# HGRN2 recurrence of a streaming encoder step: one chain over all chunks of a half in place of three chains of three chunks

## The chip, the cores and the metric

The kernel runs on one core of one Trainium2 chip. The metric is device time in microseconds (us) of one execution; the time before is the median of three runs. A profiled execution of the same program gives the trace.

## The reference, cut to what matters

One encoder layer works on a prompt of 2048 tokens and on 8 running streams of 16 tokens (128 tokens together). A projection of 1024 to 4096 columns feeds two groups: stick-breaking attention (8 heads of 64) and HGRN2, a gated linear recurrence (4 heads, key and value dimension 128). The change concerns HGRN2 alone:

```python
# per head: f = lb + (1-lb)*sigmoid(fh), k = 1 - f, q = silu(qh)
# S_t = diag(f_t) S_{t-1} + k_t outer i_t,   o_t = S_t^T q_t
def step(S, xs):                       # one chunk
    qc, kc, gc, ic = xs
    b = jnp.cumsum(gc, axis=2)         # gc = log f
    decay = jnp.where(causal, jnp.exp(b[:, :, :, None, :] - b[:, :, None, :, :]), 0.0)
    scores = jnp.einsum('bhtd,bhsd,bhtsd->bhts', qc, kc, decay)
    o = einsum('bhts,bhsv->bhtv', scores, ic) + einsum('bhtd,bhdv->bhtv', qc * exp(b), S)
    S_new = exp(b_last)[..., None] * S + einsum('bhsd,bhsv->bhdv', kc * exp(b_last - b), ic)
    return S_new, o
# then per head RMSNorm of o, times a gain and silu(gh); then the output projection and LayerNorm
```

## The kernel before, in words

The program has two stages. In the first, TensorE computes the whole input projection in two halves of the tokens: half 0 has 1024 prompt tokens and the 128 sample tokens (nine chunks of 128), half 1 the other 1024 prompt tokens (eight chunks). In the second come attention, the running streams and the output projection.

The first stage goes over `order`, a list of sections of the projection: for each head FH, QH, GH (forget gate, query, output gate of HGRN2), a few sections of the attention (KA, QA, VA, GA), and IH (HGRN2's values) for two heads at a time. A section is computed in three tiles of up to 384 tokens, each by 24 matmuls into a PSUM tile `pj` (`pe_T`, lines 311 to 318; `pe_N`, lines 320 to 328, has tokens on the output's partitions). The next section's weights are split into a high and a low part (`split_w`, line 262, called at line 681 when the first tile of a section is done): ScalarE copies, GpSimd subtracts (line 118).

When GH of a head is done (line 688), three chains are queued for it, one for each tile of three chunks (`hgrn`, lines 406 to 553). A chain is a Python generator whose `yield`s cut it into 13 steps (15 with the sample chunk). `weave` (line 608) is called between groups of 6 to 12 projection matmuls, three times a tile in `pe_T`. Each call adds `HRATE` = 1.0 to a credit (kept at 2.0 at most), and each whole credit issues one step of a chain at that place of every engine's program:

```python
credit[0] = min(credit[0] + rate, 2.0)
while credit[0] >= 1.0 and step_chain():
    credit[0] -= 1.0
```

`step_chain` (line 588) takes the first chain, issues one step and puts it back at place 1, so that the two oldest chains alternate. `drain` (line 615) finishes chains whose tiles are about to be used again. Engines run what is issued to them in order, so the places fixed by `weave` set the order of all work.

The steps of a chain: the first computes kS = 1 - f and q times f into a tile `qf` (VectorE) and clears `sc` and `sd` (GpSimd). Then come seven levels, m = 1, 2, 4, ..., 64. At a level TensorE forms products of kS and q in small blocks, 32 columns wide up to m = 16 (`near`, lines 427 to 431; the first level also forms a product `p0` with the q not yet multiplied), pairs of 32 at m = 32 and of 64 at m = 64 (line 451), into a PSUM tile `ps`. VectorE multiplies half of q and half of kS by running products of f (`tot`, lines 467 and 468), takes the scores out of `ps` (`keep`, line 434; line 461) and forms the next `tot` (line 471). The next level's products read the multiplied q and kS. A float32 matmul of the program stands as two records in the trace.

The last part: transposes of kS into `pk`, copied to `kN` (line 482); products of kN with the values into `pu` and the state's update `st`, `stt` (lines 495 to 505); the output `po` from `sc` and from `qf` with the old states (lines 510 to 518); squares on ScalarE (line 522); the root on GpSimd (`rsqrt`, line 131); the scaling on VectorE (line 528); transposes into `pq` and the gate (lines 532 and 533); the store. For the sample chunk, states of eight streams are loaded, read and updated (lines 414, 486, 518, 541 to 553).

Of the kernel before, what the change touches and what calls it, by code (L numbers as in the profile page):

```python
# [41 lines left out]
HRATE = 1.0  # L42
# [24 lines left out]
def stream_step_kernel(ctx: ExitStack, tc: tile.TileContext, x_prompt, x_sample, cache_k, cache_v, state_s,  # L67
# [131 lines left out]
    with ExitStack() as ph:  # L199
# [3 lines left out]
        hw = R("hw", 2)  # L203
# [202 lines left out]
        def hgrn(half, h, hg, t0, nch):  # L406
            n = nch * P
            smp = half == 0 and t0 + n > 1024
            npr = nch - 1 if smp else nch
            c0 = t0 // P  # L410
            q, f, g = (hg[a][:, t0:t0 + n] for a in "qfg")
            iv = lambda c: hg["i"][:, c0 + c]
# [4 lines left out]
            kS = hw.tile([P, TW], F32, name="kS", tag="kS")[:, :n]  # L417
            dve.tensor_scalar(kS, f, -1.0, 1.0, ALU.mult, ALU.add)
            sc = hw.tile([P, 3, P], F32, name="sc", tag="sc")
            sd = hw.tile([P, 3, BLK], F32, name="sd", tag="sd")  # L420
            q0, q = q, hw.tile([P, TW], F32, name="qf", tag="qf")[:, :n]
            pool.memset(sc[:, :nch], 0.0)
            pool.memset(sd[:, :nch], 0.0)
            dve.tensor_tensor(q, q0, f, ALU.mult)
            yield

            def near(ps, q, k):
                for c in range(k):
                    for s0_ in range(0, P, BLK):
                        r = slice(c * P + s0_, c * P + s0_ + BLK)  # L430
                        mm(ps[s0_:s0_ + BLK, c], kS[:, r], q[:, r], start=True, stop=True)  # L431
# [3 lines left out]

            tot = f
            tot16 = None
            for li, m in enumerate(LEVELS):
                k = nch if m < TS else npr
                bank = psc.tile([P, 4, P], F32, name="ps", tag="ps")  # L440
                ps = bank[:, :, :BLK]
                if m < BLK:
                    if li == 0:
                        p0 = bank[:, :, BLK:2 * BLK]
                        near(p0, q0, nch)
                    near(ps, q, k)
                else:
                    ps = bank
                    for c in range(k):
                        for s0_ in range(0, P, 2 * m):  # L450
                            mm(ps[s0_:s0_ + m, c, :m], kS[:, c * P + s0_:c * P + s0_ + m],
                               q[:, c * P + s0_ + m:c * P + s0_ + 2 * m], start=True, stop=True)

                def keep_scores():
                    if m < BLK:
                        if li == 0:
                            keep(p0, NL, nch)
                        keep(ps, li, k)
                        return
                    for s0_ in range(0, P, 2 * m):  # L460
                        dve.tensor_copy(sc[s0_:s0_ + m, :k, s0_ + m:s0_ + 2 * m], ps[s0_:s0_ + m, :k, :m])

                nn = k * P
                q4 = q[:, :nn].rearrange("p (b two m) -> p b two m", two=2, m=m)
                k4 = kS[:, :nn].rearrange("p (b two m) -> p b two m", two=2, m=m)
                t3 = tot[:, :nn // m].rearrange("p (b two) -> p b two", two=2)
                dve.tensor_tensor(q4[:, :, 1], q4[:, :, 1], bc(t3[:, :, 0], m), ALU.mult)
                dve.tensor_tensor(k4[:, :, 0], k4[:, :, 0], bc(t3[:, :, 1], m), ALU.mult)
                keep_scores()
                nt = hw.tile([P, TW // 2 // m], F32, name=f"tot{m}", tag=f"tot{m}")[:, :nn // (2 * m)]  # L470
                dve.tensor_tensor(nt, t3[:, :, 0], t3[:, :, 1], ALU.mult)
                tot = nt
                if m == 8:
                    tot16 = nt
                if m == BLK:
                    for s0_ in range(0, P, BLK):
                        r = slice(s0_, s0_ + BLK)
                        pool.tensor_copy(sc[r, :nch, r], sd[r, :nch])
                yield
            pk = pt.tile([P, 4, P], F32, name="pk", tag="pt")  # L480
            for c in range(nch):
                nc.tensor.transpose(pk[:, c], ch(kS, c), ident)
            kN = hw.tile([P, 3, P], F32, name="kN", tag="kN")
            act.copy(kN[:, :nch], pk[:, :nch])
            if smp:
                qz = xr.tile([P, NB, P], F32, name="qz", tag="x")
                pool.memset(qz[:, :, :2 * TS], 0.0)
                for a in range(2):
                    pool.tensor_copy(qz[:, a::2, a * TS:(a + 1) * TS],
                                     ch(q, npr).rearrange("p (b a t) -> p b a t", a=2, t=TS)[:, :, a])  # L490
            yield
            po = pho.tile([P, 4, P], F32, name="po", tag="po")
            pu = pt.tile([P, 4, P], F32, name="pu", tag="pt")
            for c in range(npr):
                mm(pu[:, c], kN[:, c], iv(c), start=True, stop=True)
            olds = []
            tmp = hw.tile([P, 2, P], F32, name="stt", tag="stt")
            cur = st[h][(c0 // 3 + 3 * half) % 3]
            for c in range(npr):
                olds.append(cur)  # L500
                new = tmp[:, c] if c < npr - 1 else st[h][(c0 // 3 + 3 * half + 1) % 3]
                if half == 0 and c0 + c == 0:
                    dve.tensor_copy(new, pu[:, c])
                else:
                    dve.scalar_tensor_tensor(new, cur, tot[:, c:c + 1], pu[:, c], ALU.mult, ALU.add)
                cur = new
            yield
            for c in range(npr):
                only = half == 0 and c0 + c == 0
                mm(po[:, c], sc[:, c], iv(c), start=True, stop=only)  # L510
                if not only:
                    mm(po[:, c], ch(q, c), olds[c], start=False, stop=True)
            if smp:
                c = npr
                mm(po[:, c], sc[:, c], iv(c), start=True, stop=True)
                for b in [*range(0, NB, 2), *range(1, NB, 2)]:
                    r = slice(b // 2 * 2 * TS, (b // 2 + 1) * 2 * TS)
                    mm(po[r, c], qz[:, b, :2 * TS], s0[:, b], start=False, stop=True, skip_group_check=True)
            ms = hw.tile([P, 4], F32, name="ms", tag="ms")
            mo = hw.tile([P, 3, P], F32, name="mo", tag="mo")  # L520
            for c in range(nch):
                act.activation(mo[:, c], po[:, c], AF.Square, accum_out=ms[:, c:c + 1])
            yield
            rs = hw.tile([P, 4], F32, name="rs", tag="rs")
            rsqrt(rs[:, :nch], ms[:, :nch], 1.0 / DG, RMS_EPS)
            yield
            on = hw.tile([P, 3, P], F32, name="on", tag="on", bufs=1)
            dve.tensor_tensor(on[:, :nch], po[:, :nch], bc(rs[:, :nch], P), ALU.mult)
            yield
            pq = pt.tile([P, 4, P], F32, name="pq", tag="pt")  # L530
            for c in range(nch):
                nc.tensor.transpose(pq[:, c], on[:, c], ident)
            dve.tensor_tensor(mo[:, :nch], pq[:, :nch], g.rearrange("p (c t) -> p c t", t=P), ALU.mult)
            mf = mo.rearrange("p c t -> p (c t)")
            for a, c, m in spans(half, t0, n):
                defer(lambda a=a, c=c, m=m: dma.dma_start(mx_d[4 + h][:, c:c + m], mf[:, a:a + m]), 2)
            if half == 1 and t0 + n == 1024:
                dma.dma_start(s_prompt[0, 0, h], st[h][(c0 // 3 + 3 * half + 1) % 3])
            if smp:
                yield  # L540
                iz = qz[:, :4]
                pool.tensor_tensor(iz, iv(npr).unsqueeze(1).to_broadcast([P, 4, P]), bc(hmask, P), ALU.mult)
                yield
                pbs = []
                for b in range(2):
                    pbs.append(psc.tile([P, 4, P], F32, name="pb", tag="ps"))
                    r = slice(b * DH, (b + 1) * DH)
                    mm(pbs[b], kN[r, npr], iz[r], start=True, stop=True)
                for b in range(NB):
                    pb = pbs[b // 4]  # L550
                    o = npr * P // TS + b
                    dve.scalar_tensor_tensor(s0[:, b], s0[:, b], tot16[:, o:o + 1], pb[:, b % 4], ALU.mult, ALU.add)
# [35 lines left out]
        def step_chain():  # L588
# [4 lines left out]
            if not done:  # L593
                chains.insert(min(1, len(chains)), g)
# [40 lines left out]
        for i, (half, sec, j) in enumerate(order):  # L635
# [52 lines left out]
            if sec == GH:  # L688
                for t0, n in TILES[half]:
                    chains.append((4 * half + j, gen1(hgrn(half, j, hg, t0, n // P))))  # L690
# [624 lines left out]
```

## Time and profile before

| | us |
|---|---|
| median of three runs | 1715.24 |
| lowest and highest run | 1713.12, 1717.34 |
| the profiled execution, its own time | 1714.12 |
| its span on the core | 1712.3 |
| TensorE matmul busy | 1646.8 |
| VectorE busy | 895.5 |
| GpSimd busy | 771.3 |
| ScalarE busy | 700.5 |

The span is the stretch from the first to the last instruction of the trace, and all windows count from its start. Busy time is the union of an engine's instructions; idle time stands with the instruction that ended it and with what that instruction waited for. The first stage reaches to about 980 us.

### The profile page before, as it was taken

The numbers are of one execution on the slowest core, as the hardware profiler recorded it, in microseconds if no ns is written. First come the engines' busy times: TensorE is split into PE (matmuls) and PEld (weight loads), VectorE is DVE, ScalarE is ACT, GpSimd is POOL, SyncE is SP. The second block draws the span as 40 slices with busy tenths as digits, with TensorE's granted clock in tenths as the row PEclk, the third lists the DMA queues.
The fourth block names the chain that finished last, engine by engine and source line by source line (L and its number), as shares of the span: only waits on it lengthen the run. The fifth ranks groups of instructions, "written<-read, shape, count | busy, mean of one in ns | idle before, by whom it ended". The sixth has DMA issues, their size and how long they took to land.

```text
span 1712.3 us, 38577 instructions
## 1 busy us (share of the span) xinstructions
PE 1646.8 (96%) x15413; PEld 1468.1 (86%) x15413; DVE 895.5 (52%) x1738; ACT 700.5 (41%) x1617; POOL 771.3 (45%) x942
## 2 busy tenths in 40 slices
PE   8999999999999999999999879999999999999998
PEld 8999999998989999999989858777787777778886
DVE  4253442245423342531554257788887777765555
ACT  3231221221223221221222257787878888874110
POOL 1242221223331332232333356776776776665664
PEclk9999999999999999999999989999999999999999
DMA  4233232122344242231123596999885854422443
GB/s 157 59 117 104 64 102 75 52 81 63 111 139 138 64 127 59 84 102 41 64 64 108 141 219 133 241 193 223 174 199 148 223 153 124 93 70 68 140 143 112
DMA packets 298811, 204.16 MB, mean 119 GB/s; under 512 B 113532, under 2 KB 275976, under 8 KB 298632
## 3 DMA queue, kind: packets, MB, share of 16 engines
q1 hardware_dynamic: 298632, 201.69, 44.4%
q8 instruction: 123, 2.02, 0.5%
q14 instruction: 56, 0.46, 0.1%
HBM read 146.06 MB, written 56.10 MB: 118 GB/s over the span
## 4 chain that ended last, share of the span: by engine, by line
PE 85%; ACT 5%; DMA 3%; DVE 3%; POOL 1%; issue 1%; SPq 0%; POOLq 0%; DVEq 0%; ACTq 0%
PE pj L314 12%; PE pj L316 10%; PE pj L315 10%; PE po L808 7%; PE z L755 6%; PE wt L790 6%; PE pj L324 4%; PE py L1145 4%; PE pj L326 4%; PE pj L325 4%; PE py L1147 4%; PE py L1146 4%; PE ps L431 2%; PE pk L890 2%; ACT keep L763 1%
## 5 line engine op out<-in xcount | busy, mean ns | idle before, releaser
L314 PE MATMUL pj<-xh,wh 128*128 128x384 f32 (+1 forms) x1152 | 399.3, 347 | 0.0
L316 PE MATMUL pj<-xh,wl 128*128 128x384 f32 (+1 forms) x1152 | 377.8, 328 | 0.0
L315 PE MATMUL pj<-xl,wh 128*128 128x384 f32 (+1 forms) x1152 | 377.3, 328 | 0.0
L777 POOL TENSOR_TENSOR s<-s,pr 128x512 f32<-128x512 f32 (+3 forms) x320 | 322.8, 1014 | 119.9 <-DVE pr L724 101.5
L118 POOL TENSOR_TENSOR wl<-wr,wh 128x512 fp32r<-128x512 f32 x126 | 164.3, 1327 | 345.6 <-ACT wh L110 320.7
L724 DVE TENSOR_TENSOR_SCAN pr<-keep,pr,one 128x513 f32<-128x513 f32 x192 | 238.4, 1269 | 49.5 <-ACT keep L763 35.9
L314 PEld LDWEIGHTS pj<-xh,wh 128*128 128x128 f32 x1152 | 217.9, 189 | 9.1 <-issue 2.9
L315 PEld LDWEIGHTS pj<-xl,wh 128*128 128x128 f32 x1152 | 218.6, 190 | 0.0
L316 PEld LDWEIGHTS pj<-xh,wl 128*128 128x128 f32 x1152 | 217.8, 189 | 0.0
L755 PE MATMUL z<-kst,qr 128*128 128x512 f32 (+3 forms) x640 | 186.5, 402 | 16.5 <-ACT keep L763 6.5
L110 ACT COPY wh<-wt 128x512 f32<-128x512 f32 (+3 forms) x320 | 166.1, 551 | 79.2 <-PE wt L790 77.9
L760 ACT ACTIVATE s<-z 128x512 f32<-128x512 f32 (+3 forms) x320 | 185.6, 580 | 12.6 <-PE z L757 9.2
L790 PE MATMUL wt<-ident,s 128*128 128x128 f32 x1088 | 166.0, 280 | 4.3 <-POOL s L777 3.9
L324 PE MATMUL pj<-wh,xh 128*128 128x256 f32 x544 | 162.1, 298 | 0.0
L790 PEld LDWEIGHTS wt<-ident,s 128*128 128x128 f32 x1088 | 124.0, 143 | 36.8 <-issue 15.5
L325 PE MATMUL pj<-wl,xh 128*128 128x256 f32 x544 | 153.7, 283 | 0.0
L326 PE MATMUL pj<-wh,xl 128*128 128x256 f32 x544 | 153.7, 283 | 0.0
L808 PEld LDWEIGHTS po<-wh,vst 128*64 128x64 f32 x2176 | 118.4, 138 | 26.1 <-issue 16.5
L118 POOL TENSOR_TENSOR e<-ev,e 128x384 fp32r<-128x384 f32 (+1 forms) x48 | 44.4, 926 | 210.7 <-ACT e L110 156.8
L755 PEld LDWEIGHTS z<-kst,qr 128*128 128x128 f32 x640 | 105.1, 196 | 38.0 <-ACT keep L763 18.6
L808 PE MATMUL po<-wh,vst 128*64 128x128 f32 x2176 | 137.7, 278 | 0.0
L763 ACT ACTIVATE keep<-z 128x512 f32<-128x512 f32 (+2 forms) x230 | 135.4, 589 | 0.0
(160 smaller groups left out, 2683.6 us busy)
## 6 DMA issues: line engine op xcount, KB each, us to landing
wr<-in_w_in SPq DMA_DIRECT2D x64, 512.0 KB
qr<-qT_d SPq DMA_DIRECT2D x64, 256.0 KB
kr<-in_cache_k SPq DMA_DIRECT2D x16, 1024.0 KB
vr<-in_cache_v SPq DMA_DIRECT2D x32, 512.0 KB
kst<-kT_d SPq DMA_DIRECT2D x24, 512.0 KB
mt<-mx_d SPq DMA_DIRECT2D x136, 64.0 KB
x<-in_x_prompt SPq DMA_DIRECT2D x16, 512.0 KB
out<-xr SPq DMA_DIRECT2D x16, 512.0 KB
```

The costliest lines, as they stand in the source:

```text
L118: eng_lo.tensor_tensor(lo, src, f32(hi), ALU.subtract)
L314: mm(o, wh[:, k], xh[:, k, :n], start=k == 0, stop=False)
L315: mm(o, wh[:, k], xl[:, k, :n], start=False, stop=False)
L316: mm(o, wl[:, k], xh[:, k, :n], start=False, stop=k == KT - 1)
L324: mm(o, xh[:, k, ts], wh[:, k], start=k == 0, stop=False)
L325: mm(o, xh[:, k, ts], wl[:, k], start=False, stop=False)
L326: mm(o, xl[:, k, ts], wh[:, k], start=False, stop=k == KT - 1)
L724: dve.tensor_tensor_scan(pr[:, CW - wd:CW + 1][:, ::-1], kr, by, carry, ALU.mult, ALU.bypass)
L755: mm(z[:, :wd], q[:, a, r, q0:q0 + P], k[:, a, k0:k0 + wd], start=r == 0, stop=r == 1 and not top)
L777: pool.tensor_tensor(s[:, :wd], s[:, :wd], pr[:, CW - wd + 1:CW + 1], ALU.mult)
L790: nc.tensor.transpose(pt_[:, x:x + P], U[(u, a)][0][:, x:x + P], ident)
L808: mm(o[r], v[:, lo // P % 8 + x, r], th[a][:, x * P:(x + 1) * P], start=top and x == 0, stop=bot and x == n - 1, skip_group_check=True)
```

## The change

Each head of each half gets one chain over all its chunks (nine in half 0, eight in half 1), where it had three chains of three chunks (the last of two in half 1). Each level is then one run of products over all chunks, and each VectorE and GpSimd instruction of a level covers all chunks. The product with the unmultiplied q gets a step of its own ahead of the levels. The last part goes in groups of three chunks in five stages (`back`, `state`, `read`, `scale`, `gate`), each group one step behind the one before it. Tiles are overwritten: q takes the place of `qf`, kS of `kN`, `sc` of `mo` and `on`, the gate tile `g` takes the output; the pool `hw` has one buffer of a tile where it had two. `step_chain` puts the chain back at the front, so that one chain is worked on until it is done. A chain has 17 steps, and `HRATE` goes from 1.0 to 0.45. The core of the diff:

```diff
-HRATE = 1.0
+HRATE = 0.45
...
-        hw = R("hw", 2)
+        hw = R("hw")
...
-        def hgrn(half, h, hg, t0, nch):
+        def hgrn(half, h, hg, nch):
             n = nch * P
...
-            kS = hw.tile([P, TW], F32, name="kS", tag="kS")[:, :n]
+            kS = hw.tile([P, 9 * P], F32, name="kS", tag="kS")[:, :n]
             dve.tensor_scalar(kS, f, -1.0, 1.0, ALU.mult, ALU.add)
...
-            dve.tensor_tensor(q, q0, f, ALU.mult)
-            yield
...
+            ps = bank(BLK)
+            near(ps, nch)
+            dve.tensor_tensor(q, q, f, ALU.mult)
+            keep(ps, NL, nch)
+            yield
             tot = f
             tot16 = None
             for li, m in enumerate(LEVELS):
                 k = nch if m < TS else npr
-                bank = psc.tile([P, 4, P], F32, name="ps", tag="ps")
-                ps = bank[:, :, :BLK]
+                ps = bank(max(m, BLK))
                 if m < BLK:
-                    if li == 0:
-                        p0 = bank[:, :, BLK:2 * BLK]
-                        near(p0, q0, nch)
-                    near(ps, q, k)
+                    near(ps, k)
...
+            groups = [(c, min(c + 3, nch)) for c in range(0, nch, 3)]
...
+            stages = (back, state, read, scale, gate)
+            for j in range(len(groups) + len(stages) - 1):
...
+                for i, (c0, c1) in enumerate(groups):
+                    if 0 <= j - i < len(stages):
+                        stages[j - i](i, c0, c1)
+                yield
...
-                chains.insert(min(1, len(chains)), g)
+                chains.insert(0, g)
...
-                for t0, n in TILES[half]:
-                    chains.append((4 * half + j, gen1(hgrn(half, j, hg, t0, n // P))))
+                chains.append((4 * half + j, gen1(hgrn(half, j, hg, 9 - half))))
```

`bank(m)` is a PSUM tile of 512 columns seen as chunks of m columns. `back` transposes three chunks of kS and copies them over kS (ScalarE); `state` has the products into `pu` and the update; `read` the output, its squares and the root (`rsqrt`) in one step; `scale` the multiplication on VectorE; `gate` the transposes, the gate and the store.

## Rows read from the trace of the kernel before

**Rows 1.** The page: busy time of all engines, and the granted TensorE clock in 40 equal slices of the span (tenths of full speed).
```profile
PE 1646.8 (96%) x15413; PEld 1468.1 (86%) x15413; DVE 895.5 (52%) x1738; ACT 700.5 (41%) x1617; POOL 771.3 (45%) x942
...
PEclk9999999999999999999999989999999999999999
```
**Rows 2.** Busy time by stretch of the span: length, then busy us and instructions of each engine, granted clock, DMA share, GB/s.
```profile
0.00:100.00 100.00, 94.09 (x829) 90.50 (x830) 37.99 (x93) 28.61 (x52) 20.42 (x27) 1.00 0.35 108
100.00:980.00 880.00, 862.92 (x8685) 812.22 (x8683) 347.02 (x1026) 202.90 (x526) 258.20 (x368) 1.00 0.30 90
980.00:1150.00 170.00, 153.02 (x1495) 125.77 (x1496) 122.61 (x148) 121.72 (x281) 114.71 (x153) 0.93 0.91 196
1150.00:1712.00 562.00, 536.79 (x4408) 439.63 (x4406) 387.88 (x472) 347.27 (x760) 377.95 (x394) 0.99 0.55 144
```
**Rows 3.** What TensorE waited for from 0 to 980 us: who for whom, us in total, times, longest.
```profile
PE ps L431 <- DVE kS L468: 7.2, 8, 1.0
PE xT L305 <- DMA x<-in_x_prompt: 5.7, 2, 5.2
PE pq L532 <- DVE on L528: 2.6, 3, 1.3
PE ps L431 <- DVE sd L434: 2.3, 2, 1.1
PE pb L548 <- POOL qz L542: 1.7, 1, 1.7
```
**Rows 4.** Timeline of TensorE around one run of small products (level m = 2, three chunks, 12 matmuls, 24 records): start us, us, instruction, count.
```profile
200.80 0.33 PE L315 MATMUL pj<-xl,wh 128*128 128x384 f32 x1
200.97 0.34 PE L316 MATMUL pj<-xh,wl 128*128 128x384 f32 x1
201.24 0.40 PE L431 MATMUL ps<-qf,kS 128*32 128x32 f32 x24
201.56 0.45 PE L314 MATMUL pj<-xh,wh 128*128 128x384 f32 x1
201.85 0.34 PE L315 MATMUL pj<-xl,wh 128*128 128x384 f32 x1
```
**Rows 5.** The same around a run of a first level, 48 records in one run.
```profile
84.11 0.34 PE L316 MATMUL pj<-xh,wl 128*128 128x384 f32 x1
84.38 0.39 PE L431 MATMUL ps<-hq,kS 128*32 128x32 f32 x24
84.59 0.42 PE L431 MATMUL ps<-qf,kS 128*32 128x32 f32 x24
84.94 0.44 PE L314 MATMUL pj<-xh,wh 128*128 128x384 f32 x1
85.22 0.34 PE L315 MATMUL pj<-xl,wh 128*128 128x384 f32 x1
```
**Rows 6.** Groups of TensorE instructions from 0 to 980 us, shapes apart: the small products of all levels up to m = 16 with qf (count, busy us, mean ns, idle before).
```profile
L431 PE MATMUL ps<-qf,kS 128*32 128x32 f32 x2688 | 46.5, 200 | 9.5 <-DVE kS L468 7.2 <-DVE sd L434 2.3
```
**Rows 7.** Timeline of TensorE around a run of level m = 64 (three chunks, 64 columns wide).
```profile
108.60 0.34 PE L316 MATMUL pj<-xh,wl 128*128 128x384 f32 x1
108.87 0.56 PE L451 MATMUL ps<-qf,kS 128*64 128x64 f32 x6
109.36 0.45 PE L314 MATMUL pj<-xh,wh 128*128 128x384 f32 x1
```
**Rows 8.** Timeline of TensorE around the transposes of kS (three chunks, all 128 columns).
```profile
112.60 0.34 PE L316 MATMUL pj<-xh,wl 128*128 128x384 f32 x1
112.79 0.49 PE L482 MATMUL pk<-ident,kS 128*128 128x128 f32 x3
113.03 0.42 PE L314 MATMUL pj<-xh,wh 128*128 128x384 f32 x1
113.29 0.33 PE L315 MATMUL pj<-xl,wh 128*128 128x384 f32 x1
```
**Rows 9.** Groups of VectorE instructions from 0 to 985 us, shapes apart: q times f, and kS = 1 - f (count, busy us, mean ns).
```profile
L424 DVE TENSOR_TENSOR qf<-hq,hf 128x384 f32<-128x384 f32 x20 | 11.0, 552 | 0.0
...
L418 DVE TENSOR_SCALAR kS<-hf 128x384 f32<-128x384 f32 x20 | 7.0, 351 | 0.0
...
L424 DVE TENSOR_TENSOR qf<-hq,hf 128x256 f32<-128x256 f32 x4 | 1.7, 419 | 0.0
```
**Rows 10.** Timeline of VectorE: one multiplication of q at a level, three chunks.
```profile
203.95 0.34 DVE L467 TENSOR_TENSOR qf<-qf,tot 128x192 f32<-128x192 f32 x1
```
**Rows 11.** Timelines from 252 to 259 us, of GpSimd (four subtractions of a weight split), VectorE (the two multiplications of a level) and TensorE (the next run, with its idle time).
```profile
251.70 5.24 POOL L118 TENSOR_TENSOR wl<-wr,wh 128x512 fp32r<-128x512 f32 x4
...
252.01 1.20 DVE L467 TENSOR_TENSOR qf<-qf,tot 128x192 f32<-128x192 f32 x1 [1.14 <-PE ps L431]
253.14 1.42 DVE L468 TENSOR_TENSOR kS<-kS,tot 128x192 f32<-128x192 f32 x1
...
254.71 0.40 PE L431 MATMUL ps<-qf,kS 128*32 128x32 f32 x24 [1.01 <-DVE kS L468]
```
**Rows 12.** Timeline of VectorE and TensorE where the first chain of a head begins: kS, and the ninth projection matmul of the section behind GH.
```profile
82.42 0.35 DVE L418 TENSOR_SCALAR kS<-hf 128x384 f32<-128x384 f32 x1
82.55 0.33 PE L316 MATMUL pj<-xh,wl 128*128 128x384 f32 x1
```

More of the change, by code (lines that the diff above doesn't have):

```diff
@@ L403, in v_store @@
             dma.dma_start(v_prompt[0, 0, 2 * j:2 * j + 4, r0:r0 + P].rearrange("h t d -> t h d"), v3)
-        def hgrn(half, h, hg, t0, nch):
+        def hgrn(half, h, hg, nch):
             n = nch * P
[L408 to L412, printed above, removed]
+            npr = 8
+            smp = nch > npr
+            q, f, g = (hg[a][:, :n] for a in "qfg")
+            iv = lambda c: hg["i"][:, c]
             ch = lambda a, c: a[:, c * P:(c + 1) * P]
@@ L416, in hgrn, with bank, near @@
                 dma.dma_start(s0, state_s[0, :, h].rearrange("b d e -> d b e"))
-            kS = hw.tile([P, TW], F32, name="kS", tag="kS")[:, :n]
+            kS = hw.tile([P, 9 * P], F32, name="kS", tag="kS")[:, :n]
             dve.tensor_scalar(kS, f, -1.0, 1.0, ALU.mult, ALU.add)
-            sc = hw.tile([P, 3, P], F32, name="sc", tag="sc")
-            sd = hw.tile([P, 3, BLK], F32, name="sd", tag="sd")
-            q0, q = q, hw.tile([P, TW], F32, name="qf", tag="qf")[:, :n]
+            sc = hw.tile([P, 9, P], F32, name="sc", tag="sc")
+            sd = hw.tile([P, 9, BLK], F32, name="sd", tag="sd")
+            pool.memset(sd[:, :nch], 0.0)
             pool.memset(sc[:, :nch], 0.0)
-            pool.memset(sd[:, :nch], 0.0)
-            dve.tensor_tensor(q, q0, f, ALU.mult)
             yield
-            def near(ps, q, k):
+            def bank(m):
+                return psc.tile([P, 512], F32, name="ps", tag="ps").rearrange("p (c j) -> p c j", j=m)
+            def near(ps, k):
                 for c in range(k):
@@ L439, in hgrn @@
                 k = nch if m < TS else npr
-                bank = psc.tile([P, 4, P], F32, name="ps", tag="ps")
-                ps = bank[:, :, :BLK]
+                ps = bank(max(m, BLK))
                 if m < BLK:
-                    if li == 0:
-                        p0 = bank[:, :, BLK:2 * BLK]
-                        near(p0, q0, nch)
-                    near(ps, q, k)
+                    near(ps, k)
                 else:
-                    ps = bank
                     for c in range(k):
                         for s0_ in range(0, P, 2 * m):
-                            mm(ps[s0_:s0_ + m, c, :m], kS[:, c * P + s0_:c * P + s0_ + m],
+                            mm(ps[s0_:s0_ + m, c], kS[:, c * P + s0_:c * P + s0_ + m],
                                q[:, c * P + s0_ + m:c * P + s0_ + 2 * m], start=True, stop=True)
[L454 to L461, printed above, removed]
                 nn = k * P
@@ L468, in hgrn @@
                 dve.tensor_tensor(k4[:, :, 0], k4[:, :, 0], bc(t3[:, :, 1], m), ALU.mult)
-                keep_scores()
-                nt = hw.tile([P, TW // 2 // m], F32, name=f"tot{m}", tag=f"tot{m}")[:, :nn // (2 * m)]
+                if m < BLK:
+                    keep(ps, li, k)
+                else:
+                    for s0_ in range(0, P, 2 * m):
+                        dve.tensor_copy(sc[s0_:s0_ + m, :k, s0_ + m:s0_ + 2 * m], ps[s0_:s0_ + m, :k])
+                nt = hw.tile([P, 9 * P // 2 // m], F32, name=f"tot{m}", tag=f"tot{m}")[:, :nn // (2 * m)]
                 dve.tensor_tensor(nt, t3[:, :, 0], t3[:, :, 1], ALU.mult)
@@ L479, in hgrn @@
                 yield
[L480 to L484, printed above, removed]
-            if smp:
[L486 to L490, printed above, removed]
@@ L491, in hgrn @@
-            yield
[L492 to L543, printed above, removed]
+            groups = [(c, min(c + 3, nch)) for c in range(0, nch, 3)]
+            cur = [st[h][half * len(groups) % 3]]
+            olds, pos, rss = {}, {}, {}
+            def back(i, c0, c1):
+                pk = pt.tile([P, 4, P], F32, name="pk", tag="pt")
+                for c in range(c0, c1):
+                    nc.tensor.transpose(pk[:, c - c0], ch(kS, c), ident)
+                act.copy(kS[:, c0 * P:c1 * P].rearrange("p (c d) -> p c d", d=P), pk[:, :c1 - c0])
@@ new lines, in state @@
+            def state(i, c0, c1):
+                pu = pt.tile([P, 4, P], F32, name="pu", tag="pt")
+                c1 = min(c1, npr)
+                for c in range(c0, c1):
+                    mm(pu[:, c - c0], ch(kS, c), iv(c), start=True, stop=True)
+                tmp = hw.tile([P, 2, P], F32, name="stt", tag="stt", bufs=2)
+                for c in range(c0, c1):
+                    olds[c] = cur[0]
+                    new = tmp[:, c - c0] if c < c1 - 1 else st[h][(half * len(groups) + i + 1) % 3]
+                    if half == 0 and c == 0:
+                        dve.tensor_copy(new, pu[:, 0])
+                    else:
+                        dve.scalar_tensor_tensor(new, cur[0], tot[:, c:c + 1], pu[:, c - c0], ALU.mult, ALU.add)
+                    cur[0] = new
@@ new lines, in read @@
+            def read(i, c0, c1):
+                po = pos[i] = pho.tile([P, 4, P], F32, name="po", tag="po")
+                for c in range(c0, c1):
+                    o = po[:, c - c0]
+                    only = half == 0 and c == 0
+                    mm(o, sc[:, c], iv(c), start=True, stop=only or c == npr)
+                    if c == npr:
+                        for b in [*range(0, NB, 2), *range(1, NB, 2)]:
+                            r = slice(b // 2 * 2 * TS, (b // 2 + 1) * 2 * TS)
+                            mm(o[r], qz[:, b, :2 * TS], s0[:, b], start=False, stop=True, skip_group_check=True)
+                    elif not only:
+                        mm(o, ch(q, c), olds[c], start=False, stop=True)
+                ms = hw.tile([P, 4], F32, name="ms", tag="ms", bufs=2)
+                for c in range(c0, c1):
+                    act.activation(sc[:, c], po[:, c - c0], AF.Square, accum_out=ms[:, c - c0:c - c0 + 1])
+                rs = rss[i] = hw.tile([P, 4], F32, name="rs", tag="rs", bufs=2)
+                rsqrt(rs[:, :c1 - c0], ms[:, :c1 - c0], 1.0 / DG, RMS_EPS)
@@ new lines, in scale, with gate @@
+            def scale(i, c0, c1):
+                dve.tensor_tensor(sc[:, c0:c1], pos[i][:, :c1 - c0], bc(rss[i][:, :c1 - c0], P), ALU.mult)
+            def gate(i, c0, c1):
+                pq = pt.tile([P, 4, P], F32, name="pq", tag="pt")
+                for c in range(c0, c1):
+                    nc.tensor.transpose(pq[:, c - c0], sc[:, c], ident)
+                mo = g[:, c0 * P:c1 * P]
+                m3 = mo.rearrange("p (c t) -> p c t", t=P)
+                dve.tensor_tensor(m3, pq[:, :c1 - c0], m3, ALU.mult)
+                for a, c, m in spans(half, c0 * P, (c1 - c0) * P):
+                    defer(lambda a=a, c=c, m=m: dma.dma_start(mx_d[4 + h][:, c:c + m], mo[:, a:a + m]), 2)
+                if half == 1 and c1 == npr:
+                    dma.dma_start(s_prompt[0, 0, h], cur[0])
@@ new lines, in hgrn @@
+            stages = (back, state, read, scale, gate)
+            for j in range(len(groups) + len(stages) - 1):
+                if j == 0 and smp:
+                    qz = xr.tile([P, NB, P], F32, name="qz", tag="x")
+                    pool.memset(qz[:, :, :2 * TS], 0.0)
+                    for a in range(2):
+                        pool.tensor_copy(qz[:, a::2, a * TS:(a + 1) * TS],
+                                         ch(q, npr).rearrange("p (b a t) -> p b a t", a=2, t=TS)[:, :, a])
+                if j == 5 and smp:
+                    iz = qz[:, :4]
+                    pool.tensor_tensor(iz, iv(npr).unsqueeze(1).to_broadcast([P, 4, P]), bc(hmask, P), ALU.mult)
+                for i, (c0, c1) in enumerate(groups):
+                    if 0 <= j - i < len(stages):
+                        stages[j - i](i, c0, c1)
+                yield
@@ L547, in hgrn @@
                     r = slice(b * DH, (b + 1) * DH)
-                    mm(pbs[b], kN[r, npr], iz[r], start=True, stop=True)
+                    mm(pbs[b], ch(kS, npr)[r], iz[r], start=True, stop=True)
                 for b in range(NB):
-                    pb = pbs[b // 4]
                     o = npr * P // TS + b
-                    dve.scalar_tensor_tensor(s0[:, b], s0[:, b], tot16[:, o:o + 1], pb[:, b % 4], ALU.mult, ALU.add)
+                    dve.scalar_tensor_tensor(s0[:, b], s0[:, b], tot16[:, o:o + 1], pbs[b // 4][:, b % 4],
+                                             ALU.mult, ALU.add)
                 defer(lambda: dma.dma_start(s_sample[0, :, h].rearrange("b d e -> d b e"), s0), 2)
```

## The prediction

> **What bounds the kernel now.** I read the page first: TensorE is busy for 96% of the span, VectorE for 52%, at the full granted clock nearly throughout [rows 1]. Then the busy time by stretch, since an average hides stages [rows 2]. From 100 to 980 us, where the chains of HGRN2 run beside the projection, TensorE is busy 862.9 of 880 us at clock 1.00; VectorE stands at 347, GpSimd at 258, ScalarE at 203, DMA at a share of 0.30. This stage is TensorE's alone: what shortens its in-order program by a microsecond shortens the stage by about one, and work taken from the others gives nothing by itself. The change touches only this stage. From 980 to 1150 us DMA is at 0.91, but these loads are issued behind the first stage, so that they move with its end. Third, who TensorE waits for up to 980 us [rows 3]: the chains make it wait 7.2 + 2.3 + 2.6 + 1.7 = 13.8 us; 5.7 us are for x at the two starts and stay.
>
> "Busy" says nothing of what a run of small products costs, so I read the timeline around single runs. Projection matmuls start 0.17 us apart (200.80, 200.97). A run of 24 records sits between the matmul at 200.97 and the second one behind it at 201.85: 0.88 us where two steps of 0.173 would do, so it costs 0.53 us [rows 4]. A run of 48 costs 85.22 - 84.11 - 0.35 = 0.76 us [rows 5]. The 24 further records cost 0.23 us, 0.0096 each, and what is left of 0.53 is a fixed 0.30 us a run. It can be seen where it lies: the run starts 0.27 instead of 0.17 us behind the last projection matmul, and the second projection matmul behind it comes 0.29 us after the first. Three transposes on all 128 columns cost 113.29 - 112.60 - 0.35 = 0.34 us, 0.11 each, the distance of a plain stream [rows 8]: no fixed part. So it comes with entering and leaving narrow blocks, not with every change of work.
>
> The Trainium skill has two rules here, on its page "TensorEngine Tiling (Array Packing)". "Key Properties" says that a change of tiling mode drains the engine: a cost for each run, as the rows show. "Instruction Overhead" speaks against the change: it puts about 60 cycles on each matmul, however small, which joining runs would not save; estimated from it, a record at 2.4 GHz would cost 25 ns, a run of 24 0.6 us and one of 48 1.2 us. The first is near the row, the second is not.
>
> **The change part by part.**
> *Runs joined.* A head had three chains with seven runs each, 21; it gets one run ahead of the levels and seven levels, 8. Over 8 heads (four in each half) 168 runs become 64. The number of small matmuls stays, so the records stay (2688 of them read `qf` [rows 6]). 104 runs x 0.30 = 31.2 us go. For m = 32 and 64 I take the same fixed part: a run of six wide records starts 0.27 us behind the projection and costs 109.36 - 108.60 - 0.17 + 0.11 = 0.70 us [rows 7], more for each record and no sign of another entry cost. The records' slope is measured to 48 and used to 72; a twofold slope beyond 48 would cost 24 x 0.0096 = 0.23 us on some 48 runs, 11 us (a rival).
>
> *The last part.* Its transposes, products and outputs are the same matmuls on 128 columns (0.11 us a piece [rows 8]), so joining them gives nothing. The copies over kS and q, fewer tiles and wider memsets are on engines with room: nothing. What hides them is the projection; where VectorE is late, TensorE waits, and that is the next term.
>
> *The waits of today* (13.8 us) go with the chains that make them; others come.
>
> *Waits inside a level.* A level's products need q and kS of the level before. One multiplication of 192 elements takes 0.34 us [rows 10]; the slope of the same operation is (552 - 419) / 128 = 1.04 ns an element [rows 9], so with 576 it takes 0.34 + 384 x 0.00104 = 0.74 us, two of them 1.48, with the handover some 1.6 us from the end of a run. At a rate of 0.45 steps come two or three `weave` calls apart, at the least 15 projection matmuls, 2.6 us. So 1.0 us is spare, and an undisturbed level costs nothing (in the tiles of 256 tokens of half 1, about a fifth, the spare is near 0.3).
>
> VectorE is disturbed where GpSimd subtracts for the next weights: during four of these the two multiplications took 1.20 and 1.42 us for 0.34 each, and TensorE then stood for 1.01 us [rows 11]. Each waits for a GpSimd instruction to end (5.24 / 4 = 1.31 us), whatever its own length. So such a level is late by 1.20 + 1.42 - 0.68 = 1.9 us, 0.9 more than is spare. How often? Counting credits from the start of a chain, m = 1 is issued three calls behind the first step, in the second tile of the section, just behind the next weights' split, and so again m = 16 in the next section (for one head of a half it is a later level). That is two levels a head, 16 in all: 14 us, and 2 more where four subtractions follow instead of two: 16 us. The ends: 5 if the splits mostly miss the multiplications, 34 if the 16 lose 1.6 us each and ten others 0.8.
>
> *The start of a chain.* A full credit issues the first two steps at once, so the first run wants all of kS at once. Now kS of one chain starts at 82.42, and the ninth matmul of the section at 82.55 [rows 12]; the run could begin 0.27 behind, at 82.82. With 1152 columns kS takes between 0.35 (as with 384 [rows 9]) and 1.05 us; I take 0.76, between these, since twice the columns of q f do not take twice the time. It is there at 83.2, 0.4 us late; in half 1, with tiles of 256 ahead, less. Eight starts: 2.5 us (0 to 6).
>
> *The last part's waits.* Today gate and states' update make TensorE wait 2.6 + 1.7 us [rows 3]. The new form has the output, squares and root in one step and the scaling in the next: from output to gate two steps in place of three, some 4.4 `weave` calls for 6, and VectorE waits for the root with the next group's update behind it. I put 4 us (0 to 10).
>
> The sum, against the profiled execution's 1714.12: - 31.2 - 13.8 + 16 + 2.5 + 4 = -22.5, so 1691.6. The median of the runs is 1.1 above that execution; such a difference I don't carry. 1692 us.
>
> **The rivals.**
> 1. *VectorE uncovered at every level (slower).* One chain has no second one beside it: TensorE can't do another chain's run while this one's multiplications are late, and each of 56 levels waits. At the 1.01 us of [rows 11] each, 56 us of waits stand against 31.2 + 13.8 = 45 us gained: with starts and last part 1714.1 - 45 + 56.6 + 6.5 = 1732 us. From 0.7 us a level on (39 + 6.5) nothing is won. For it: those two waits stand in one split, 2.9 us apart. Against it: GpSimd is busy only 29% of this stage [rows 2], and the spare is 1.0 us elsewhere. Chance 0.12, in half of which it only uses up the gain (1710 to 1720).
> 2. *No fixed part to save.* If the cost of a long run grows with its records, a run of 72 costs three of 24 (1.59 us instead of 0.99): 1714.1 - 13.8 + 22.5 = 1723 us; at the twofold slope beyond 48, 1703. Against it: 24 and 48 records [rows 4, 5]. The Trainium skill, "TensorEngine Tiling (Array Packing)", "Instruction Overhead", has this rival's rule. Chance 0.05 for the full form.
> 3. *Waits go altogether.* A third of the VectorE instructions means a third of the occasions to stand behind GpSimd, and the levels could mostly slip through: waits of 7 in all, 1714.1 - 45 + 7 = 1676 us. Against it: the split is issued right ahead of two levels a head. Chance 0.10.
> 4. *It doesn't do what it says:* with one buffer in `hw` a chain would wait for the one before, or be left over at `drain` and run uncovered. A chain needs 17 / 0.45, less the credit saved, some 35 calls, and between two heads' GH lie 45 and more. Chance 0.03, time as rival 1.
>
> **How the numbers follow.** The forecast has 0.70: all low ends at once would give 1674 us, all high ones 1719; as they will hardly fall together, 1680 to 1708 for itself. Time 1692. The range takes in half of rival 3 and the near form of rival 2, 1676 to 1710: outside lie rivals 1, 2 and 4 (0.20 less the near halves) and a few hundredths below. A measurement of this kernel tells 0.3%, 5 us, from no change. Faster than 1710: the forecast, rival 3 and a little of 1, 0.83. Within 5 us: the middle of rival 1, 0.07. Slower: the rest of 1, 2 and 4, 0.10.
>
> **What would show it.** Right: single runs of 72 (half 0) or 64 records where 24 stood, each costing 0.9 to 1.0 us, and 64 narrow runs; busy time from 100 us to the stage's end down by about 30; TensorE's waits for kS behind GpSimd's subtractions, at about 1 us, some 16 times; waits for kS at a chain's start of a few tenths. The second stage as long as before. Wrong: a run of 72 at 1.5 us (rival 2), waits at levels with no GpSimd instruction beside them (rival 1), a chain's steps without projection between them (rival 4), or a stage of attention that begins earlier and does not end earlier.

## The result, and the profile after

The changed kernel takes 1672.15 us (median of four runs, 1670.32 to 1676.21) against 1714.78 us (1713.12 to 1717.34) beside it: ratio 0.9753, 95% interval 0.9731 to 0.9775. Timed once more beside other kernels it gave 1676.89 against 1712.56, 0.9784 (0.9767 to 0.9801). The forecast of 1692 us (1676 to 1710) had the direction and the place; the first timing lies below its range, the second just inside it. Line numbers below are those of each run's own kernel.

The page, and busy time by stretch (columns as in [rows 2]). The stretches are cut where the same stages end: 940 and 1110 us stand where 980 and 1150 stood.
```profile
PE 1606.8 (96%) x15413; PEld 1455.2 (87%) x15413; DVE 835.1 (50%) x1226; ACT 701.3 (42%) x1617; POOL 770.2 (46%) x846
```
```profile
100.00:940.00 840.00, 826.27 (x8637) 802.23 (x8635) 286.09 (x537) 203.95 (x527) 255.84 (x274) 1.00 0.32 94
940.00:1110.00 170.00, 153.77 (x1501) 125.94 (x1501) 123.77 (x149) 123.14 (x284) 115.70 (x154) 0.94 0.92 198
1110.00:1669.00 559.00, 534.47 (x4400) 437.37 (x4400) 387.08 (x470) 346.00 (x758) 377.20 (x394) 1.00 0.56 144
```
TensorE has as many records as before (15413), 40 us less busy time, and nearly all of that in the first stage. VectorE does 537 instructions there for 1026, 61 us less; TensorE stays the bound, so that these 61 us are not time saved.

A run of level m = 2 in the timeline of TensorE, for [rows 4]:
```profile
204.61 0.33 PE L315 MATMUL pj<-xl,wh 128*128 128x384 f32 x1
204.78 0.34 PE L316 MATMUL pj<-xh,wl 128*128 128x384 f32 x1
205.05 0.83 PE L431 MATMUL ps<-hq,kS 128*32 128x32 f32 x72
205.81 0.45 PE L314 MATMUL pj<-xh,wh 128*128 128x384 f32 x1
206.09 0.34 PE L315 MATMUL pj<-xl,wh 128*128 128x384 f32 x1
```
It costs 206.09 - 204.78 - 0.35 = 0.96 us, as forecast (0.99) and not 3 x 0.53. It starts 0.27 us behind the last projection matmul, and the second projection matmul behind it comes 0.28 us after the first, where 0.17 is usual; a run of 24 had the same. The late exit shows in a group too, for the first of three projection matmuls (`pj`, line 314) over the whole span, before (first fence) and after:
```profile
L314 PE MATMUL pj<-xh,wh 128*128 128x384 f32 (+1 forms) x1152 | 399.3, 347 | 0.0
```
```profile
L314 PE MATMUL pj<-xh,wh 128*128 128x384 f32 (+1 forms) x1152 | 386.6, 336 | 0.0
```
It is the one behind a run. Its busy time falls by 12.7 us, that of the other two (lines 315 and 316) by 1.8 and 1.9.

What TensorE waits for up to 945 us, for [rows 3] (line 458 multiplies kS, line 417 makes it):
```profile
PE ps L431 <- DVE kS L458: 4.9, 8, 1.0
PE ps L451 <- DVE kS L458: 2.2, 3, 1.4
...
PE ps L431 <- issue: 1.7, 2, 1.5
PE ps L431 <- DVE kS L417: 1.5, 4, 0.4
```
The chains make it wait 4.9 + 2.2 + 1.7 + 1.5 = 10.3 us (the 1.7 are stops inside runs, see the last section), less than the 13.8 of before; I had 22.5. Nothing of the last part is in the list; its groups (line 525 the gate's transposes, line 554 the streams' update) had no idle time ahead:
```profile
L525 PE MATMUL pq<-ident,sc 128*128 128x128 f32 x68 | 11.3, 272 | 0.0
...
L554 PE MATMUL pb<-qz,kS 64*128 64x512 f32 x16 | 4.5, 641 | 0.0
```

A level that waits and one that doesn't. First m = 1 of the first head: GpSimd, VectorE, and TensorE's next run.
```profile
88.43 3.05 POOL L118 TENSOR_TENSOR wl<-wr,wh 128x512 fp32r<-128x512 f32 x2
...
88.69 1.65 DVE L457 TENSOR_TENSOR hq<-hq,hf 128x576 f32<-128x576 f32 x1 [3.37 <-PE ps L431]
90.26 1.84 DVE L458 TENSOR_TENSOR kS<-kS,hf 128x576 f32<-128x576 f32 x1
...
92.25 0.82 PE L431 MATMUL ps<-hq,kS 128*32 128x32 f32 x72 [0.44 <-DVE kS L458]
```
Then m = 16 of the same head, just behind the next split:
```profile
107.17 3.42 POOL L118 TENSOR_TENSOR wl<-wr,wh 128x512 fp32r<-128x512 f32 x2
...
106.92 0.83 DVE L457 TENSOR_TENSOR hq<-hq,tot 128x512 f32<-128x512 f32 x1 [3.49 <-PE ps L431]
107.68 1.78 DVE L458 TENSOR_TENSOR kS<-kS,tot 128x512 f32<-128x512 f32 x1
...
109.64 0.70 PE L451 MATMUL ps<-hq,kS 128*32 128x32 f32 x32
```
Both multiplications are late in the first, by 0.9 and 1.1 us over the 0.74 to 0.76 of an undisturbed one, and TensorE stands for 0.44. In the second only kS is late, by 1.1 us over the 0.69 of an undisturbed one of 512 columns; the two calls' worth of projection cover it, and the run has no idle time ahead.

### The profile page after: what moved, and what is told of

Same layout as the page of the kernel before. It is cut to its first block, busy times and chain, and to the rows that moved or that the text cites. A ratio compares the mean times of both kernels' runs of the same rounds, so it can differ in the third digit from the quotient of the medians.

```text
span 1669.7 us, 37776 instructions
## 1 busy us (share of the span) xinstructions
PE 1606.8 (96%) x15413; PEld 1455.2 (87%) x15413; DVE 835.1 (50%) x1226; ACT 701.3 (42%) x1617; POOL 770.2 (46%) x846
## 4 chain that ended last, share of the span: by engine, by line
PE 85%; ACT 4%; DVE 4%; DMA 3%; issue 1%; SPq 1%; POOL 1%; POOLq 0%; DVEq 0%
PE pj L314 11%; PE pj L316 10%; PE pj L315 10%; PE po L813 7%; PE z L760 6%; PE wt L795 6%; PE pj L324 4%; PE pj L326 4%; PE py L1150 4%; PE pj L325 4%; PE py L1152 4%; PE py L1151 4%; PE ps L431 2%; PE pk L895 2%; DVE kS L458 1%
## 5 line engine op out<-in xcount | busy, mean ns | idle before, releaser
L314 PE MATMUL pj<-xh,wh 128*128 128x384 f32 (+1 forms) x1152 | 386.6, 336 | 0.0
L118 POOL TENSOR_TENSOR wl<-wr,wh 128x512 fp32r<-128x512 f32 x126 | 171.4, 1384 | 345.9 <-ACT wh L110 344.7
L324 PE MATMUL pj<-wh,xh 128*128 128x256 f32 x544 | 158.7, 292 | 0.0
L332 ACT ACTIVATE sg<-pj 128x384 f32<-128x384 f32 (+1 forms) x72 | 34.1, 474 | 224.4 <-PE pj L316 217.3
```

Source lines behind the costliest of these rows:

```text
L314: mm(o, wh[:, k], xh[:, k, :n], start=k == 0, stop=False)
L324: mm(o, xh[:, k, ts], wh[:, k], start=k == 0, stop=False)
```

## The experiments

My theory after the result: narrow runs have a fixed cost that joining saves, and waits come where a level's place meets a subtraction of GpSimd. The rivals: runs cost by their records; a level waits for its own length anywhere.

**Runs broken up again.** In the changed kernel, `full()` is a transpose of the identity into unused columns of the level's own PSUM tile (`raw[0]`).
```diff
+            def full():
+                nc.tensor.transpose(raw[0][:, 384:512], ident, ident)
...
                 for c in range(k):
+                    if c in (3, 6):
+                        full()
                     for s0_ in range(0, P, BLK):
```
(the same at m = 32)

> The changed kernel, with two extra transposes of the identity (128 columns, into unused columns of the same PSUM tile, read by nobody) inside each run of small products up to m = 32, behind the third and the sixth chunk: 7 runs x 2 x 8 heads = 112 of them. A transpose costs 0.11 us by itself. Theory A (a run has a fixed 0.30 us for entering and leaving narrow blocks): 112 x (0.11 + 0.30) = 46 us over the changed kernel, some 1718 us. Theory B (a run costs by its records, nothing for the entry): 112 x 0.11 = 12 us, 1684.

And its control, with both transposes behind the run:
```diff
                         mm(ps[s0_:s0_ + BLK, c], kS[:, r], q[:, r], start=True, stop=True)
+                for _ in range(2):
+                    full()
```

> The control: the same 112 transposes, but both behind the run that they were put into, where it is left anyway. Theory A: 112 x 0.11 = 12 us, 1684 us, some 34 us less than with the transposes between the chunks. Theory B: 1684, the same as with the transposes between.

Between: 1707.89 us, ratio to before 0.9968 (0.9958 to 0.9979). Behind: 1682.98 us, 0.9819 (0.9799 to 0.9839). The same instructions are 24.9 us dearer between than behind; a run of 72 with its surroundings, between (first fence) and behind:
```profile
201.34 0.34 PE L316 MATMUL pj<-xh,wl 128*128 128x384 f32 x1
201.60 0.40 PE L439 MATMUL ps<-hq,kS 128*32 128x32 f32 x24
201.93 0.33 PE L431 MATMUL ps<-ident 128*128 128x128 f32 x1
202.19 0.40 PE L439 MATMUL ps<-hq,kS 128*32 128x32 f32 x24
202.51 0.33 PE L431 MATMUL ps<-ident 128*128 128x128 f32 x1
202.77 0.40 PE L439 MATMUL ps<-hq,kS 128*32 128x32 f32 x24
203.10 0.44 PE L314 MATMUL pj<-xh,wh 128*128 128x384 f32 x1
203.38 0.34 PE L315 MATMUL pj<-xl,wh 128*128 128x384 f32 x1
```
```profile
199.47 0.34 PE L316 MATMUL pj<-xh,wl 128*128 128x384 f32 x1
199.74 0.83 PE L437 MATMUL ps<-hq,kS 128*32 128x32 f32 x72
200.50 0.44 PE L431 MATMUL ps<-ident 128*128 128x128 f32 x2
200.69 0.42 PE L314 MATMUL pj<-xh,wh 128*128 128x384 f32 x1
200.95 0.34 PE L315 MATMUL pj<-xl,wh 128*128 128x384 f32 x1
```
1.69 against 1.13 us without waits: 0.28 for each break, 31 us for 112. The times were expected 34 us apart and differ by 24.9, in part since the kernel with breaks also waits less for chains and inside runs (4.7 against 9.1 us). Theory A holds, with 0.28 for 0.30; B is out. The Trainium skill's "TensorEngine Tiling (Array Packing)", "Key Properties", says that a change of mode drains the engine; the trace agrees in that a change costs time, 0.28 us in and out.

**One chain alive, alone.** The kernel before with one edit:
```diff
-                chains.insert(min(1, len(chains)), g)
+                chains.insert(0, g)
```

> The kernel before with one part of the change alone: the chain that was stepped goes back to the front, so that one chain is alive, still three chains of three chunks a head at a rate of 1.0. A level then has one call's worth of projection (1.0 to 1.6 us) to finish in. Theory A (a level waits where its two multiplications, 0.34 us each and up to 1.3 us more behind a GpSimd subtraction, are not over by the next run): more waits than the 13.8 us of before, by 15 to 40 us, 1730 to 1755 us; so the step spacing that the lower rate keeps is what makes the changed kernel's waits small. Theory B (having one chain alive costs nothing as such): 1715.

1740.58 us, ratio 1.0158 (1.0127 to 1.0188): this part by itself is a loss of 27 us. What TensorE waits for up to 1000 us:
```profile
PE ps L431 <- DVE kS L468: 22.0, 24, 1.8
PE pq L532 <- DVE on L528: 6.9, 7, 2.1
...
PE pb L548 <- POOL qz L542: 1.7, 1, 1.7
PE pk L482 <- DVE kS L468: 1.6, 3, 0.6
PE ps L431 <- DVE qf L424: 1.3, 2, 0.6
```
33.5 us, where the same rows had 14.2 before (the 13.8 of [rows 3] and 0.4 at line 482), with waits at levels and gates: 19 of the 27 us. Theory A; the other 8 us are not assigned.

**The kernel before, again.**

> The kernel before once more, for its profile: the first stage of the changed kernel's projection matmuls next to each other took 3.4 us less than before and the second stage 2.1 us less, which nothing in the change explains. Theory A (these are the spread of single executions): a second profile differs from the first by as much, 2 to 4 us in either term. Theory B (they belong to the change): the same as in the first profile within 0.5 us.

One execution of 1716.13 us. From the starts of the last projection matmul in the timelines (977.03 and 974.80 us before, 936.55 after) and the spans (1712.3, 1714.3, 1669.7) the second stage lasts 735.3 and 739.5 us before, and 733.1 after (736.1 in a second profile of after). Projection matmuls next to each other lost 3.6 us against their usual distance in the first profile and 0.8 in the second; 0.2 after, and 2.7 in that second profile. So single executions differ by 3 to 4 us in either term (theory A), and I count neither as the change's.

**Places and lengths.** Four kernels beside each other: the changed one, and it with one edit each.

> The changed kernel once more, beside the next three: 1672 us, and TensorE's waits for the chains in the trace at 10 us (7 at the levels, 1.5 at the starts of chains, under 2 of a stop inside a run that the profile puts down to nothing). If that last stop is chance, it stands elsewhere or nowhere in this profile.

1676.89 us, 5 more than expected. The waits on kS were the same within 0.3 us (5.1, 2.3 and 1.5), the stops inside runs 3.9 us for 1.7.

```diff
-                    split(act, dve if i == 0 and e else pool, hi[:, ks], lo[:, ks], r[:, kr])
+                    copy(act, hi[:, ks], r[:, kr])
+                    eng = dve if i == 0 and e else pool
+                    for z in range(2):
+                        u = n // 2 * z
+                        zs, zr = slice(ks.start + u, ks.start + u + n // 2), slice(kr.start + u, kr.start + u + n // 2)
+                        eng.tensor_tensor(lo[:, zs], r[:, zr], f32(hi[:, zs]), ALU.subtract)
```

> The changed kernel with each subtraction of a weight split in two instructions of half the length (256 instead of 512 elements a partition); nothing else moves. Theory A (a level waits because each of its multiplications stands until a whole GpSimd subtraction is over, some 1.1 to 1.3 us): that stretch falls to some 0.6 us, the multiplications behind it from 1.78 us to 1.3 or less, the levels' waits from 7 us to 3 or less, 1668 us. Theory B (GpSimd only takes a share of the port): multiplications and waits as long as before, 1672 or, with the second instruction's own cost, more.

1667.50 us, ratio 0.9740 (0.9725 to 0.9755), 9.4 us below its neighbour. The place of m = 1 again (GpSimd, then VectorE), and the waits on kS:
```profile
88.84 4.37 POOL L282 TENSOR_TENSOR wl<-wr,wh 128x256 fp32r<-128x256 f32 x4
...
89.09 1.10 DVE L462 TENSOR_TENSOR hq<-hq,hf 128x576 f32<-128x576 f32 x1 [3.40 <-PE ps L436]
90.12 1.29 DVE L463 TENSOR_TENSOR kS<-kS,hf 128x576 f32<-128x576 f32 x1
```
```profile
PE ps L436 <- DVE kS L422: 1.5, 4, 0.4
...
PE ps L436 <- DVE kS L463: 0.7, 2, 0.4
PE pk L488 <- DVE kS L463: 0.4, 1, 0.4
```
1.65 and 1.84 us became 1.10 and 1.29; the levels' waits fell from the neighbour's 7.4 us to 0.9 (0.7 in the fence and 0.2 at line 456, m = 64). Where no VectorE instruction runs beside it, a subtraction takes 1.29 us and a half one 0.74 (medians of these two traces): 0.55 less, as the multiplications. So a multiplication stands until one whole subtraction is over, and theory A holds. The Trainium skill says the same ("SBUF — State Buffer", "SBUF: two separate sides": the port pair that VectorE and GpSimd share is locked for a whole instruction); the trace agrees, by 0.55 us for half an instruction. Of the 9.4 us, 3.7 are fewer stops inside runs (0.2 for 3.9), which no run ties to the halves; beside the changed kernel's first timing the intervals overlap.

```diff
             pool.memset(sc[:, :nch], 0.0)
             yield
+            yield
```

> The changed kernel with an empty step behind the first one, so that all later steps of a chain come one place later. Theory A (waits come where a level's place falls on a split of weights, and at a start because the first run wants kS at once): the 1.5 us at the starts go, the run of m = 1 moves away from the split and its 0.4 to 1.0 us go, while other levels may meet one; 4 to 8 us of waits, 1668 to 1671 us. Theory B (every level waits for its own length, wherever it is): as before, 1672.

1663.35 us, ratio 0.9709 (0.9696 to 0.9722); once more 1663.41 us, 0.9716. Waits for the chains:
```profile
PE ps L452 <- DVE kS L459: 2.2, 3, 1.4
...
PE ps L432 <- DVE kS L459: 0.4, 1, 0.4
```
The waits at the starts are gone, and of the 4.9 us at the runs up to m = 16 only 0.4 are left. Theory A, though the time is 5 us below its range: against the neighbour, waits on kS and stops inside runs are 9.6 us less, the time 13.5.

> The changed kernel with a rate of 0.40 instead of 0.45: more steps come three calls apart instead of two, and 17 steps still end ahead of the next drain. Theory A (a level has about 1.0 us to spare at two calls, and 1.0 to 1.6 more at three): the levels' waits fall to about half, 1668 to 1671 us. Theory B (places alone decide): other levels meet the splits, and the sum stays at 7, 1672.

1671.66 us, ratio 0.9758 (0.9744 to 0.9771): levels' waits of 4.4 + 2.1 us for the neighbour's 7.4. They did not fall to half: on the waits B was right, a slower rate hardly lowers them. The time is 5.2 us below the neighbour's, but the intervals overlap, and 2.7 us of it are fewer stops inside runs.

> The changed kernel with a rate of 0.60 instead of 0.45: a third of the steps then come one call apart (1.0 to 1.6 us of projection) and the others two. Theory A (a level needs some 1.6 us from the end of its run, so two calls leave 1.0 us to spare and one call nothing): the levels' waits rise from 7 us to 15 to 35 us, 1680 to 1700 us. Theory B (waits come only where GpSimd subtracts): 5 to 12 us of waits, 1670 to 1676 us.

This one was timed later, beside the two kernels below: 1675.50 us, ratio 0.9785 (0.9771 to 0.9798). Waits at the levels:
```profile
PE ps L431 <- DVE kS L458: 5.5, 6, 1.6
...
PE ps L451 <- DVE kS L458: 2.4, 2, 1.2
```
Again B, with its numbers: a level one call behind the last is just ready. From a run's start to the end of its kS an undisturbed level takes 2.1 to 2.3 us, and in this trace one call brings the next run in 2.0 to 2.5. Seven of the eight waits stand behind a multiplication that met a subtraction of GpSimd; the eighth, 0.31 us, stands behind an undisturbed level.

**Shift and halves together.**

> The empty step behind the first one and the halved subtractions together. With the empty step alone 3.2 us of waits for the chains were left, 2.6 of them on kS behind GpSimd. Theory A (those too last as long as one subtraction): the 2.6 us fall to under 1, and the time is 1 to 2 us below the empty step alone, 1662 us, if the longer GpSimd program costs nothing. Theory B (what halving gave was chance): no difference, or slower.

> The kernel with the empty step alone once more, beside the one with both: 1663 us, with 2 to 4 us of waits for the chains.

1660.79 us, ratio 0.9697 (0.9683 to 0.9711), with 0.2 us of waits on kS left (theory A on the waits); the shift alone 1663.41, 0.9716 (0.9701 to 0.9731). The intervals of the two overlap, so the further 2.6 us are not settled; both are faster than the changed kernel.

## Why the prediction was wrong

*The bound, right.* TensorE's in-order program in the first stage: 40.5 of the 42.6 us between the two spans are there, and the other 2.2 are within what the second stage differs by between executions.

*Runs joined, right.* 31.2 us forecast. Taking the time between neighbouring projection matmuls beyond their usual 0.174 or 0.119 us for every run of both timelines, the 168 and the 64 narrow runs differ by 36.0 us; 13 runs of `kn` transposes (0.33 us each) that stood beside narrow runs before and stand alone now belong to it with the other sign, and waits are 0.8 us more: 32.5 us. All runs with full-width work, apart from waits, cost 2 us less, where I had nothing.

*The waits, the step that failed.* I took away 13.8 us and put 22.5 in their place; it became 10.3. Three terms: "Waits inside a level", 16 us, measured 7.1, or 8.8 with the stops inside runs. The 16 levels were where I said, behind the splits, but I gave each the lateness of [rows 11], where both multiplications meet a subtraction. So it was at m = 1 in seven of the eight chains, with waits of 0.4 to 1.0 us, 4.2 in all; the eighth had one late there, and waited 0.7 us a level later. At m = 16 at most one of the two met one, and its 1.1 us are no more than the spare. The three waits at line 451 (2.2 us) came behind m = 32, two of them where four subtractions stood and both multiplications met one. "The last part's waits", 4 us, measured 0: I set the calls between output and gate against each other (4.4 for 6) without comparing them with what the work between takes. "The start of a chain", 2.5 us, measured 1.5, 0.34 to 0.43 each and only in half 0.

These add to 12.2 us of the 20 between 1692 and 1672; 1.3 are the joined runs, 2 the full-width ones. The remaining 4 to 5 are within what single executions differ by (the other timing of the changed kernel was 4.7 us longer). That this other timing falls just inside the range is luck and nothing of the terms: its waits on kS were the same, its stops longer. The range ended at rival 3's 1676, which has fewer waits and every other term as forecast; there was no room for fewer waits and small gains elsewhere at once.

*The rivals.* Rival 1 (uncovered levels) is real where one chain steps at a rate of 1.0 (27 us lost), not at 0.45. Rival 2 fell. Rival 3 was nearest. Rival 4 didn't occur.

## What to carry to other kernels

Between full-width matmuls, a run of small products in narrow blocks pays for entering and leaving; join such runs until waits for the joined step cost more, and price both from single places in the timeline. Cost a wait at each place by itself: one bad place multiplied by a count of similar ones overstated it more than twofold here (16 us for 7.1). Where one engine locks out another for a whole instruction, shorter instructions or another place of meeting can help; both lowered the waits here (7.4 to 0.9 us, and to 2.6).

## What the runs showed that was not expected

Long runs stop inside, and the profile names no cause. The last head's run of m = 4, after (first fence) and in its second profile:
```profile
864.67 0.60 PE L431 MATMUL ps<-hq,kS 128*32 128x32 f32 x46
866.80 0.35 PE L431 MATMUL ps<-hq,kS 128*32 128x32 f32 x18 [1.53 <-issue]
```
```profile
869.43 0.60 PE L431 MATMUL ps<-hq,kS 128*32 128x32 f32 x46
872.16 0.35 PE L431 MATMUL ps<-hq,kS 128*32 128x32 f32 x18 [2.13 <-issue]
```
Both stop behind the 46th of 64 records, by 1.5 and 2.1 us; no narrow run of the two profiles before shows such a stop. The second profile has one more, of 1.57 us in the sixth chain's run of m = 8 (at 681.6 us), that the first has not. From 863 to 866 us in the first, the DMA queues are full:
```profile
q1 hardware_dynamic: 1783, 0.94, 105.1%
q8 instruction: 1, 0.02, 2.1%
```
Full queues are not needed for a stop: from 679.5 to 682 us in the second profile they are busy for 16%. What the stops share is a transfer of instructions. All 15 stops inside narrow runs or just behind one, in eight profiles of after and its variants, end 2.2 to 2.7 us after the start of a transfer on q8; its transfers have 16384 bytes, and there are 122 of them, one for some 126 of the 15413 records. A kernel timed twice (the empty step alone) stops behind the same record both times, by 0.56 and 0.55 us. This speaks for an instruction supply that comes late when a run eats its instructions in 0.6 us. The Trainium skill ("Runtime: NRT & Kernel Launch", "Instruction fetch mechanics") calls the crossing from one block of instructions to the next mostly hidden; here, if this is what it is, it isn't always. No run tried it by itself, so the cause stays argued.
